# Encoder block on one core: joints of the MLP reordered and rotary angles behind the second unit of v

## The chip, the cores and the metric

The kernel runs on one core of a Trainium2 chip. The metric is the device time of one execution in microseconds (us); a lower number is better. The engines are named as the profile names them: PE is TensorE, DVE is VectorE, ACT is ScalarE, POOL is GpSimd, SP is SyncE, which here only issues DMAs.

## The reference

One encoder block over 1,024 tokens of width 1,024, in float32. `neighborhood_attention` and `dilated_attention` are softmax attentions; only the parts around the change are kept here.

```python
a = rms_norm(h, g_mix)
qa, ka, va, qd, kd, vd, gate_na, gate_dil = split(a @ w_in)
y_na  = neighborhood_attention(qa, ka, va, rpb)
y_dil = dilated_attention(rotary(qd, positions), rotary(kd, positions), vd)
mixed = sigmoid(gate_na) * (y_na @ w_branch_na) + sigmoid(gate_dil) * (y_dil @ w_branch_dil)
h = h + mixed @ w_out
c = rms_norm(h, g_mlp)
h = h + square(relu(c @ w_up)) @ w_down
e = rms_norm(h, g_ple)
h = h + sigmoid(e @ w_ple_gate) * (p @ w_ple_proj)
out = rms_norm(h, g_final)
```

## The kernel before, in words

Every matrix product is made of three passes: an operand is split into a high part (a cast on ACT, L109) and a low part (source minus high part, a subtraction on DVE or POOL, L110), and `mm3` (L206) issues high x high, high x low and low x high (profile lines L208 to L210). Weights stream through a ring of buffers (`w_raw`, `w_hi`, `w_lo`). The large products are done in blocks with seven products in place of eight: sums and differences of blocks (t1 to t4, on POOL) stand beside plain blocks (b11, b21, b22). The scheduler of the framework orders each engine's instructions from the program order, from priorities and from buffer releases; inside an engine they run in that order.

**Token tiles and v.** At the start eight token tiles of 128 rows are normalised (`norm_to_act`; L239 to L248 are small steps of the reciprocal square root, L258 writes `xn`), transposed on PE through two PSUM tiles `tp` (L275) and split into `act`. Behind them stand five units of the v projection (`v_unit`, PSUM `ps_v`, output `v_stage`). Between the tiles the rotary angles are made on DVE (L349 to L375: position times frequency, reduced to one turn by twelve steps at L358) and ACT (two Sin, L376 and L377); they are stored to `cs_scr` for the rotary step much later.

**Out-projection and first MLP product.** For each of eight token tiles, the loop at L1131 loads a row of x into `hx` (L1132), makes two halves of `mixed @ w_out` (24 matmuls each, PSUM `ps_t`), adds them (L1137) and sums squares on ACT (L234). `norm_to_ops` (L1093) of the tile before is issued behind the first half: it normalises, transposes, and for tiles 4 to 7 makes the left operands of the first MLP product: x (L1112, L1114), s2 (L1115), and two differences on POOL in `keep` (L1118, L1119), which is loaded from `c_scr` (L1106). All these are split into act10, act11, s2, s3, s4. Heads of units 0 and 1 of W_up (`fast_head`, L177: blocks b11 and b21, tile `f_raw`) and the sums of unit 0 (`fast_sums`, L183 load, L186 to L189 on POOL) are issued in the last tile. Then the loop over 16 units of W_up (L1230) makes per unit seven products of 12 matmuls (PSUM `pp`): b11 and b21, which read only tiles 0 to 3 (act00, act01), and t1, t2, t3, b22, t4, which need all tiles.

**Second MLP product.** Seven chunks of W_down (L1352 on), each seven products of four PSUM tiles `ps_d` with six matmuls each, in the order `DOWN` = b11, b21, t1, t2, t3, b22, t4. Left blocks come from `l_scr` into four places (`load_left`, L1288: two halves of `u_raw` and two of an `h` tile), right blocks from W_down (`load_right`, L1296; POOL sums at L1303). `operands` splits them for the next chunk behind each product. In chunk 0 the products b11, t1, t2, t3 are copied out of PSUM by ACT (L1339); all else is added on DVE (L1341). In the last chunk the results are combined (L1345, DVE and POOL), and the left operand of the four last units of W_up's output is split from `u_raw`: first half loaded early (L1365), the second half into the same buffer at L1380, behind the splits of the first.

**Tail.** The gate product of the last token tile is done in two pieces of 256 columns (L1434 on); each goes through `gated` (L1418 to L1423: sigmoid, times p, plus h, square), then the final norm and the store (L1454).

Of the kernel before, what the change touches and what calls it, by code (L numbers as in the profile page):

```python
# [9 lines left out]
F32 = mybir.dt.float32  # L10
# [49 lines left out]
def encoder_kernel(ctx: ExitStack, tc: tile.TileContext, t: dict, out: bass.AP):  # L60
# [236 lines left out]
    with ExitStack() as st:  # L297
# [41 lines left out]

        pi = qp.tile([P, 256], I32, name="pi", tag="rt")  # L340
        for a in range(4):
            nc.sync.dma_start(pi[a * 32:(a + 1) * 32],
                              t["positions"][:, a * 256:(a + 1) * 256].broadcast_to((32, 256)))
        invf = qp.tile([P, 1], F32, name="invf", bufs=1)
        nc.sync.dma_start(invf, t["invf"])
        hpi = qp.tile([P, 1], F32, name="hpi", bufs=1)
        nc.vector.memset(hpi, float(np.pi / 2))
        r, k1, k2, ab, sn, cn = (qp.tile([P, 256], F32, name=n_, tag="rt") for n_ in "abcdef")
        nc.vector.tensor_copy(r, pi)  # L349
        nc.vector.tensor_scalar(r, r, invf, None, op0=ALU.mult)  # L350
        big = 4096.0 * TWO_PI
        nc.vector.tensor_scalar(k1, r, 1.0 / big, MAGIC, op0=ALU.mult, op1=ALU.add)
        nc.vector.tensor_scalar(k1, k1, MAGIC, None, op0=ALU.subtract)
        cp = _fixed_parts(big, [2.0 ** (8 - 7 * i) for i in range(8)])
        pp = _fixed_parts(TWO_PI, [2.0 ** (-9 - 12 * i) for i in range(3)])

        def less(k, part, dst=r):
            nc.vector.scalar_tensor_tensor(dst, k, -part, r, op0=ALU.mult, op1=ALU.add)  # L358

        for i in range(3):  # L360
            less(k1, cp[i])
        less(k1, cp[3], k2)
        nc.vector.tensor_scalar(k2, k2, 1.0 / TWO_PI, MAGIC, op0=ALU.mult, op1=ALU.add)
        nc.vector.tensor_scalar(k2, k2, MAGIC, None, op0=ALU.subtract)
        less(k2, pp[0])
        less(k1, cp[3])
        less(k2, pp[1])
        less(k1, cp[4])
        less(k1, cp[5])
        less(k2, pp[2])  # L370
        less(k1, cp[6])
        less(k1, cp[7])
        lim = float(np.nextafter(np.float32(np.pi), np.float32(0)))
# [4 lines left out]
        for i, src in enumerate((cn, sn)):  # L378
            nc.sync.dma_start(cs_scr[i].rearrange("a f n -> (a f) n"), src)
# [42 lines left out]
        for u in range(5):  # L422
            v_unit(u)
            if u < 4:
                s1.append(left_sums(u))
# [1129 lines left out]
```

## Time and profile before

| what | value |
|---|---|
| runs | 1649.92, 1651.51, 1652.97 us; median 1651.51 us |
| profiled execution | 1654.93 us, of which the span in the trace 1653.1 us |
| PE | busy 1561.5 us, 94% of the span, 7787 instructions |
| DVE, ACT, POOL | busy 72%, 43%, 39% |
| mean granted clock of PE | 0.979 |
| DMA | 277.12 MB, mean 168 GB/s |

The profiled execution is one more run; its time is its span and 1.83 us around it. A window of the trace gives for a stretch of time how long each engine was busy and the clock that PE was granted (1.00 is 2.4 GHz, 0.50 would be 1.2 GHz throughout). A timeline gives single instructions with the idle time before them and what ended it.

### The profile page before, as it was taken

Reading aid. Unit: us, or ns where it says so; the run is one execution under the profiler, and the core shown is the slowest. Engines: PE = TensorE matmul, PEld = TensorE weight load, DVE = VectorE, ACT = ScalarE, POOL = GpSimd, SP = SyncE. Lnnn points to the kernel's source line nnn. Section 1 sums busy time; section 2 is a strip of 40 time slices with the busy share of each in tenths; the row PEclk is TensorE's granted clock in tenths of the full one; section 3 lists DMA queues with packets and bytes.
Section 4 is the critical chain, followed back from the end, with each engine's and each line's share of the span. In section 5 each row is a group of like instructions: output and inputs, shape, how many; then the busy total and the mean of one; then the engine's idle time right before and its main releaser. Section 6 shows DMA issues by size and latency. Waiting matters only on the chain. (4 is left out here: it accounts for less than half of the span.)

```text
span 1653.1 us, 22585 instructions
## 1 busy us (share of the span) xinstructions
PE 1561.5 (94%) x7787; PEld 1308.2 (79%) x7787; DVE 1193.6 (72%) x2081; ACT 708.4 (43%) x1327; POOL 652.6 (39%) x434
## 2 busy tenths in 40 slices
PE   8899999999999998889997899999989999999997
PEld 6899777787888877667786688888867788887886
DVE  6744799734666877655458777777778999999855
ACT  7322222226888755654234333333345333323422
POOL 0233578613333222234214677777733322325100
PEclk9999999999999999999998899999999999999999
DMA  8552455675676777655343344444467444434122
GB/s 295 175 152 102 126 167 162 202 259 204 207 215 225 237 240 241 182 179 162 127 166 115 115 140 147 141 147 149 162 234 267 156 163 143 153 102 139 35 101 71
DMA packets 114482, 277.12 MB, mean 168 GB/s; under 512 B 14176, under 2 KB 30528, under 8 KB 113856
## 3 DMA queue, kind: packets, MB, share of 16 engines
q1 hardware_dynamic: 108608, 265.19, 48.9%
q10 hardware_dynamic: 5760, 10.49, 1.7%
q8 instruction: 62, 1.02, 0.2%
q14 instruction: 52, 0.43, 0.1%
HBM read 185.57 MB, written 90.06 MB: 167 GB/s over the span
## 5 line engine op out<-in xcount | busy, mean ns | idle before, releaser
L109 ACT CAST w_hi<-w_raw 128x512 fp32r<-128x512 f32 (+2 forms) x103 | 83.7, 826 | 137.9 <-POOL w_raw L470 56.0
L110 POOL TENSOR_TENSOR w_lo<-w_raw,w_hi 128x512 fp32r<-128x512 f32 (+2 forms) x33 | 64.3, 1951 | 162.0 <-ACT w_hi L109 117.6
L110 DVE TENSOR_TENSOR f_lo<-f_raw,f_hi 128x512 fp32r<-128x512 f32 x80 | 81.6, 1037 | 49.2 <-ACT f_hi L109 48.6
L110 DVE TENSOR_TENSOR w_lo<-w_raw,w_hi 128x1024 fp32r<-128x1024 f32 (+1 forms) x70 | 84.2, 1209 | 36.1 <-ACT w_hi L109 35.8
L722 POOL TENSOR_SCALAR s_sb<-s_sb,rs 128x384 f32<-128x384 f32 x64 | 40.0, 626 | 136.6 <-DVE rs L721 69.1
L110 DVE TENSOR_TENSOR pt_l<-tp_p,pt_h 128x384 fp32r<-128x384 f32 (+3 forms) x120 | 65.1, 542 | 27.0 <-ACT pt_h L109 25.6
L109 ACT CAST f_hi<-f_raw 128x512 fp32r<-128x512 f32 x80 | 46.2, 614 | 79.8 <-DMA f_raw<-w_up 75.7
L109 ACT CAST pt_h<-tp_p 128x384 fp32r<-128x384 f32 (+3 forms) x120 | 56.2, 469 | 33.5 <-PE tp_p L731 27.2
L1178 POOL TENSOR_TENSOR u_t<-u_t 128x512 f32<-128x512 f32 x45 | 53.2, 1183 | 39.9 <-ACT u_t L1177 38.7
L1177 ACT ACTIVATE u_t<-u_t 128x512 f32<-128x512 f32 x45 | 28.4, 631 | 74.5 <-DVE u_t L1164 74.1
L628 POOL TENSOR_TENSOR k_lo<-k_lo,k_st 128x1024 fp32r<-128x1024 f32 x12 | 32.1, 2678 | 65.0 <-ACT k_st L625 47.0
L1341 DVE TENSOR_TENSOR h<-ps_d,h 128x512 f32<-128x512 f32 x84 | 54.7, 681 | 2.4 <-PE ps_d L210 2.2
L110 DVE TENSOR_TENSOR f_lo<-f_t,f_hi 128x512 fp32r<-128x512 f32 x32 | 51.3, 1608 | 1.8
L637 PE MATMUL sc<-k_st,q_st 128*128 128x384 f32 (+3 forms) x160 | 52.3, 327 | 0.2 <-DVE stats L655 0.2
L638 PE MATMUL sc<-k_lo,q_st 128*128 128x384 f32 (+3 forms) x160 | 49.1, 307 | 2.7 <-POOL k_lo L628 2.7
L657 ACT ACTIVATE s_sb<-s_sb,stats 128x256 f32<-128x256 f32 (+2 forms) x96 | 44.9, 469 | 14.9 <-DVE stats L655 14.4
L731 PE MATMUL tp_p<-ident,s_sb 128*128 128x128 f32 x192 | 33.9, 288 | 17.1 <-POOL s_sb L722 15.1
L647 ACT ACTIVATE s_sb<-s_sb,nm 128x384 f32<-128x384 f32 x64 | 39.5, 617 | 23.8 <-DVE nm L646 19.6
L1341 DVE TENSOR_TENSOR sum_t<-ps_d,sum_t 128x512 f32<-128x512 f32 x72 | 46.8, 682 | 2.9 <-PE ps_d L210 2.9
L731 PEld LDWEIGHTS tp_p<-ident,s_sb 128*128 128x128 f32 x192 | 25.1, 147 | 29.9 <-POOL s_sb L722 20.4
L210 PE MATMUL ps_d<-w_hi,m_op 128*128 128x512 f32 x112 | 44.3, 405 | 2.6 <-DVE m_op L110 2.6
L644 DVE CUSTOM_DVE_ANT_0 s_sb<-bias,sc 128x384 f32<-128x384 f32 x64 | 35.1, 548 | 15.8 <-PE sc L638 14.1
(482 smaller groups left out, 5809.1 us busy)
## 6 DMA issues: line engine op xcount, KB each, us to landing
f_raw<-w_up SPq DMA_DIRECT2D x32, 512.0 KB
w_raw<-w_in SPq DMA_DIRECT2D x26, 512.0 KB
u_raw<-l_scr SPq DMA_DIRECT2D x25, 512.0 KB
qk_scr<-o SPq DMA_DIRECT2D x96, 128.0 KB
h<-l_scr SPq DMA_DIRECT2D x24, 512.0 KB
l_scr<-u_t SPq DMA_DIRECT2D x42, 256.0 KB
l_scr<-u_s SPq DMA_DIRECT2D x42, 256.0 KB
w_raw<-w_qk SPq DMA_DIRECT2D x20, 512.0 KB
```

The source lines that it names most:

```text
L109: nc.scalar.copy(hi, src)
L110: eng.tensor_tensor(lo, src, hi.bitcast(F32), op=ALU.subtract)
L210: nc.tensor.matmul(ps, sl, mh, start=False, stop=last)
L637: pe(nc.tensor.matmul(o, qs[:, qsl], kk, start=True, stop=False))
L638: pe(nc.tensor.matmul(o, qs[:, qsl], ll, start=False, stop=True))
L644: nc.vector.tensor_tensor_reduce(s_[:, :n], bias, sc[:, :n], 1.0, -3.0e38, op0=ALU.subtract, op1=ALU.max, accum_out=mx)
L647: nc.scalar.activation(s_[:, :n], s_[:, :n], AF.Exp, bias=nm, scale=1.0, accum_out=sm)
L657: nc.scalar.activation(s_[:, :n], s_[:, :n], AF.Exp, bias=nm, scale=-1.0, accum_out=sm)
L722: nc.gpsimd.tensor_scalar(pr, pr, rs, 1.0, op0=ALU.mult, op1=ALU.mult)
L731: pe(nc.tensor.transpose(tp[:, i * P:(i + 1) * P], pr[:, kb * P:(kb + 1) * P], ident))
L1178: nc.gpsimd.tensor_tensor(c, c, c, op=ALU.mult)
L1341: nc.vector.tensor_tensor(d, ps, d, op=ALU.add)
```

## The change

Five pieces:

1. The angle block becomes a function `angles()` and is called behind unit 1 of v.
2. The last two token tiles of the out-projection are done by halves: tile 6 first half, tile 7 first half, then the second halves. The loads of W_up's heads stand before the second halves; `keep` of tile 7 and the raw second half of unit 0 go to two free buffers of the ring (`spare`); tiles 6 and 7 keep x in `hx`. The two last `norm_to_ops` get a higher priority, and the sums of unit 0 (`fast_sums`) come behind them. The products b11 of units 0 and 1 are issued first, then both b21.
3. Chunk 0 of the second product has the order b11, b21, b22, t1, t2, t3, t4; left blocks are loaded in that order, and the operands of chunk 1 are issued as soon as their buffers' products of chunk 0 are issued, in the order `DOWN`.
4. The second half of the last four units' output (`u_scr[2:4]`) is loaded into `m_ops[0]` behind b11 of the last chunk.
5. The last token tile's gate product is cut at 384 + 128 columns.

```diff
@@ angles: the block from "pi = qp.tile" to the stores of cs_scr, L340 to L379, becomes a function
+        def angles():
...
+            nc.vector.tensor_copy(r, pi)
...
         for u in range(5):
             v_unit(u)
+            if u == 1:
+                angles()
             if u < 4:
                 s1.append(left_sums(u))
@@ norm_to_ops
-            keep = pool.tile([P, D], F32, name="keep", tag="keep")
-            nc.sync.dma_start(keep, c_scr[r])
+            if tt == NT - 1:
+                keep = spare[0]
+            else:
+                keep = pool.tile([P, D], F32, name="keep", tag="keep")
+                nc.sync.dma_start(keep, c_scr[r])
...
-            x = xn if tt == NT - 1 else ring.tile([P, D], F32, name="x_op", tag="w_raw", bufs=2)
+            x = h if tt >= NT - 2 else ring.tile([P, D], F32, name="x_op", tag="w_raw", bufs=2)
@@ out-projection
+            def half_row(tt, n):
+                hx, parts = sums[tt]
+                ps = tok_product(w8, tt, n)
+                c = slice(n * HALF, (n + 1) * HALF)
+                nc.vector.tensor_tensor(hx[:, c], ps, hx[:, c], op=ALU.add)
+                parts.append(square_part(np_, hx[:, c], ps))
+                if n == 1:
+                    nc.sync.dma_start(h_scr[tt * P:(tt + 1) * P, :], hx)
+                    before.append((hx, g, tt, parts))
...
+            load_row(NT - 2)
+            half_row(NT - 2, 0)
+            norm_to_ops(np_, op_, *before.pop())
+            load_row(NT - 1)
+            half_row(NT - 1, 0)
+            heads = [fast_head(u) for u in range(2)]
+            spare = [ring.tile([P, D], F32R, name=f"w_{b}", tag=f"w_{b}").bitcast(F32) for b in ("hi", "lo")]
+            nc.sync.dma_start(spare[0], c_scr[3])
+            half_row(NT - 2, 1)
+            with tc.high_priority(offset=150):
+                norm_to_ops(np_, op_, *before.pop())
+                half_row(NT - 1, 1)
+                norm_to_ops(np_, op_, *before.pop())
+            late = fast_sums(0, heads[0], spare[1], op_.tile([P, D], F32, name="f_t", tag="keep"))
@@ first product, loop over units
+                if u == 0:
+                    p1[0], p1[1] = head_1(0), head_1(1)
+                    for v in range(2):
+                        head_2(v, p1[v])
                 fast_rest(heads[u], *late)
-                if u == 0:
-                    p1[0] = head(0)
...
-                if u < 14:
+                if 0 < u < 14:
                     p1[u + 1] = head(u + 1)
@@ second product
+        first_order = ("b11", "b21", "b22", "t1", "t2", "t3", "t4")
+        seq = [(0, o) for o in first_order] + [(c, o) for c in range(1, 7) for o in DOWN]
...
-            for o in DOWN:
+            due = list(DOWN)
+            for o in DOWN if c else first_order:
                 down_product(o, c == 0)
                 if c < 6:
-                    operands(c + 1, o)
+                    done = first_order[:first_order.index(o) + 1] if c == 0 else (o,)
+                    while due and due[0] in done:
+                        operands(c + 1, due.pop(0))
                     continue
-                if o == "b21":
+                if o == "b11":
+                    u_more = m_ops[0].bitcast(F32).rearrange("p (f n) -> p f n", f=2)
+                    nc.sync.dma_start(u_more, u_scr[2:4].rearrange("f p n -> p f n"))
+                elif o == "b21":
...
-                        if q:
-                            nc.sync.dma_start(u_raw, u_scr[2:4].rearrange("f p n -> p f n"))
...
-                                split(hi, lo, u_raw[:, k, half * HALF:(half + 1) * HALF].rearrange(
+                                split(hi, lo, (u_more if q else u_raw)[:, k, half * HALF:(half + 1) * HALF].rearrange(
@@ last token tile
-                for a in range(2):
-                    ps = ps_mm.tile([P, HALF], F32, name="ps_t", tag="mm")[:, :256]
-                    mm_tok(ps, w8[4:], tt, slice(a * 256, (a + 1) * 256))
+                for a, b in ((0, 384), (384, HALF)):
+                    ps = ps_mm.tile([P, HALF], F32, name="ps_t", tag="mm")[:, :b - a]
+                    mm_tok(ps, w8[4:], tt, slice(a, b))
```

The scheduler turns this into another order on the engines. Three places follow, before and then after; numbers behind a name tell buffers apart.

DVE, the middle of the token tiles: `act10l` and `act11l` are low parts of a transposed tile; L349 to L375 before (L369 to L395 after) are angles.

```order
L244 TENSOR_SCALAR nv<-nv 128x1
L358 SCALAR_TENSOR_TENSOR a<-b,a 128x256
L110 TENSOR_TENSOR w_lo<-w_raw,w_hi 128x1024
L248 SCALAR_TENSOR_TENSOR ny<-nw,ny 128x1
L247 SCALAR_TENSOR_TENSOR nw<-ny,nv 128x1
L358 SCALAR_TENSOR_TENSOR a<-b,a 128x256
L110 TENSOR_TENSOR act10l<-tp,act10h 128x512
L247 SCALAR_TENSOR_TENSOR nw<-ny,nv 128x1
L248 SCALAR_TENSOR_TENSOR ny<-nw,ny 128x1
```

```order
L247 SCALAR_TENSOR_TENSOR nw<-ny,nv 128x1
L258 SCALAR_TENSOR_TENSOR xn<-x,ny,gain 128x512 x2
L248 SCALAR_TENSOR_TENSOR ny<-nw,ny 128x1
L110 TENSOR_TENSOR w_lo<-w_raw,w_hi 128x1024
L110 TENSOR_TENSOR act10l<-tp,act10h 128x512
L242 TENSOR_SCALAR ny<-nv 128x1
L247 SCALAR_TENSOR_TENSOR nw<-ny,nv 128x1
L110 TENSOR_TENSOR act11l<-tp,act11h 128x512
L110 TENSOR_TENSOR v_stage<-ps_v,v_stage 128x8x64
```

The steps at L358 are gone from between the tiles; `angles()` starts 31 rows further down, behind a `v_stage` row of unit 1.

POOL, the joint of out-projection and first MLP product: L1118 and L1119 (L1124 and L1125 after) are the differences of a token tile, s_8965 that of tile 5, s_9069 and s_9088 those of tile 6; `f_raw_9112` is unit 0's second raw half before (`w_lo` after), `f_raw_9379` and `f_raw_9378` unit 1's.

```order
L1118 TENSOR_TENSOR keep<-keep,s_8965 128x512
L1119 TENSOR_TENSOR keep<-keep,x_op 128x512
L110 TENSOR_TENSOR s4l<-keep,s4h 128x512
L1118 TENSOR_TENSOR keep<-keep,s_9069 128x512
L1119 TENSOR_TENSOR keep<-keep,x_op 128x512
L110 TENSOR_TENSOR s4l<-keep,s4h 128x512
L186 TENSOR_TENSOR f_t<-f_raw_9112,f_raw 128x512
L186 TENSOR_TENSOR f_t<-f_raw_9379,f_raw 128x512
L187 TENSOR_TENSOR f_t<-f_raw_9112,f_t 128x512
L188 TENSOR_TENSOR f_raw_9112<-f_raw_9112 128x512
L187 TENSOR_TENSOR f_t<-f_raw_9379,f_t 128x512
L188 TENSOR_TENSOR f_raw_9379<-f_raw_9379 128x512
```

```order
L1124 TENSOR_TENSOR keep<-keep,s_8965 128x512
L1125 TENSOR_TENSOR keep<-keep,x_op 128x512
L110 TENSOR_TENSOR s4l<-keep,s4h 128x512
L186 TENSOR_TENSOR f_t<-f_raw_9378,f_raw 128x512
L187 TENSOR_TENSOR f_t<-f_raw_9378,f_t 128x512
L188 TENSOR_TENSOR f_raw_9378<-f_raw_9378 128x512
L189 TENSOR_TENSOR f_raw<-f_raw,f_t 128x512
L1124 TENSOR_TENSOR keep<-keep,s_9088 128x512
L1125 TENSOR_TENSOR keep<-keep,hx 128x512
L110 TENSOR_TENSOR s4l<-keep,s4h 128x512
L1124 TENSOR_TENSOR w_hi<-w_hi,s_9159 128x512
L1125 TENSOR_TENSOR w_hi<-w_hi,hx 128x512
```

The four sums of unit 1 moved ahead of the differences of tiles 6 and 7; the sums of unit 0 moved behind them (the row `f_t<-w_lo` follows the last one shown).

DVE, chunk 0 of the second product: L1341 (L1376 after) adds a product to its sum, `h_11724` and `h_11723` being the sum of b21, `h_11724` after that of b22.

```order
L110 TENSOR_TENSOR act11h<-u_raw,act11h 128x1024
L110 TENSOR_TENSOR act10h<-h_11723,act10h 128x1024
L110 TENSOR_TENSOR act00h<-h_11723,act00h 128x1024
L1341 TENSOR_TENSOR h_11724<-ps_d,h_11724 128x512 x4
L110 TENSOR_TENSOR m_op_11731<-u_raw,m_op_11731 128x1024
L110 TENSOR_TENSOR act10l<-t_raw,act10l 128x1024
L110 TENSOR_TENSOR w_lo<-w_raw,w_hi 128x1024
```

```order
L110 TENSOR_TENSOR act11h<-h_11722,act11h 128x1024
L110 TENSOR_TENSOR act10h<-h_11722,act10h 128x1024
L1376 TENSOR_TENSOR h_11723<-ps_d,h_11723 128x512 x4
L1376 TENSOR_TENSOR h_11724<-ps_d,h_11724 128x512 x4
L110 TENSOR_TENSOR m_op_11730<-u_raw,m_op_11730 128x1024
L110 TENSOR_TENSOR act11l<-pair,act11l 128x1024
L110 TENSOR_TENSOR w_lo<-w_raw,w_hi 128x1024
```

The four additions of b22 stand directly behind those of b21, ahead of the splits for chunk 1.

## Rows read from the trace of the kernel before

**Rows 1.** windows with the busy time of each engine (instructions), the granted clock, DMA share, GB/s.

```profile
core 0: us, PE busy (x) PEld busy (x) DVE busy (x) ACT busy (x) POOL busy (x), PEclk, DMA share, GB/s
40.00:70.00 30.00, 24.64 (x183) 23.97 (x182) 26.03 (x68) 11.54 (x21) 5.00 (x3) 0.89 0.42 133
100.00:130.00 30.00, 30.00 (x252) 30.00 (x252) 13.88 (x17) 8.86 (x14) 14.02 (x9) 1.00 0.47 151
886.00:938.00 52.00, 34.40 (x123) 25.92 (x122) 42.44 (x52) 22.02 (x40) 32.06 (x22) 0.80 0.32 106
1217.00:1268.00 51.00, 44.80 (x177) 35.60 (x176) 40.98 (x35) 28.58 (x37) 19.86 (x7) 0.90 0.70 258
1268.00:1290.00 22.00, 19.66 (x79) 14.09 (x78) 22.00 (x23) 10.56 (x11) 5.67 (x2) 1.00 0.65 218
1490.00:1510.00 20.00, 16.20 (x64) 12.59 (x62) 20.00 (x21) 3.44 (x6) 18.68 (x11) 0.91 0.38 140
```

**Rows 2.** waits of PE over the span: total us, times, longest us.

```profile
PE pp L208 <- ACT f_hi L109: 8.2, 1, 8.2
...
PE ps_d L208 <- DVE h L1341: 5.8, 4, 3.5
PE tp L275 <- DVE act10l L110: 5.3, 1, 5.3
PE pp L208 <- ACT act10h L109: 5.0, 1, 5.0
```

**Rows 3.** timeline of DVE, token tiles: start us, length us, operation, [idle before <-releaser].

```profile
39.43 0.29 DVE L349 CAST a<-pi 128x256 f32<-128x256 int32 x1 [1.04 <-DMA pi<-positions]
...
45.49 0.41 DVE L358 SCALAR_TENSOR_TENSOR a<-b,a 128x256 f32<-128x256 f32 x1
45.83 0.14 DVE L243 TENSOR_SCALAR ny<-ny 128x1 int32<-128x1 int32 x1
...
58.21 0.68 DVE L110 TENSOR_TENSOR act10l<-tp,act10h 128x512 fp32r<-128x512 f32 x1
```

**Rows 4.** timeline of SP (q: a DMA issue) around the joint of W_out and W_up.

```profile
871.36 0.33 SPq L1132 DMA_DIRECT2D hx<-x  x1
...
886.24 0.42 SPq L177 DMA_DIRECT2D f_raw<-w_up  x1
```

**Rows 5.** timeline of DVE, same stretch.

```profile
883.33 1.41 DVE L258 SCALAR_TENSOR_TENSOR xn<-hx,ny,gain 128x512 f32<-128x512 f32 x2
...
900.64 3.45 DVE L258 SCALAR_TENSOR_TENSOR xn<-hx,ny,gain 128x512 f32<-128x512 f32 x2
```

**Rows 6.** timeline of POOL, same stretch.

```profile
899.31 2.53 POOL L186 TENSOR_TENSOR f_t<-f_raw,f_raw 128x512 f32<-128x512 f32 x2 [2.15 <-DVE nw L247]
...
918.32 1.28 POOL L1118 TENSOR_TENSOR keep<-keep,s 128x512 f32<-128x512 f32 x1 [6.33 <-DVE s L1115]
```

**Rows 7.** timeline of PE, same stretch.

```profile
916.14 0.79 PE L208 MATMUL pp<-act10h,f_hi 128*128 128x512 f32 x1 [4.99 <-ACT act10h L109]
...
934.75 0.39 PE L208 MATMUL pp<-act11h,f_hi 128*128 128x512 f32 x1
...
937.47 0.39 PE L208 MATMUL pp<-act00h,f_hi 128*128 128x512 f32 x1
```

**Rows 8.** timeline of DVE, first chunk of the second product.

```profile
1240.54 2.48 DVE L1341 TENSOR_TENSOR h<-ps_d,h 128x512 f32<-128x512 f32 x4
1247.28 1.23 DVE L110 TENSOR_TENSOR m_op<-u_raw,m_op 128x1024 fp32r<-128x1024 f32 x1 [4.26 <-ACT m_op L109]
```

**Rows 9.** timeline of DVE, end of the second product.

```profile
1486.93 1.28 DVE L110 TENSOR_TENSOR act00l<-u_raw,act00h 128x512 fp32r<-128x512 f32 x2
...
1501.92 1.75 DVE L110 TENSOR_TENSOR act00l<-u_raw,act00h 128x512 fp32r<-128x512 f32 x1
```

**Rows 10.** timeline of ACT, last token tile.

```profile
1639.00 0.60 ACT L1418 ACTIVATE sg<-ps_t 128x512 f32<-128x512 f32 x1 [2.63 <-PE ps_t L210]
...
1644.75 0.38 ACT L1418 ACTIVATE sg<-ps_t 128x256 f32<-128x256 f32 x1 [0.91 <-PE ps_t L210]
```

More of the change, by code (lines that the diff above doesn't have):

```diff
@@ L337, in encoder_kernel @@
             norm_to_act(qp, two(xs[tt]), g, tt, xn=qp.tile([P, D], F32, name="xn", tag="nat"))
[L340 to L373, printed above, removed]
-        nc.vector.tensor_scalar(r, r, lim, -lim, op0=ALU.min, op1=ALU.max)
-        nc.vector.scalar_tensor_tensor(ab, r, -1.0, r, op0=ALU.mult, op1=ALU.max)
-        nc.scalar.activation(sn, r, AF.Sin)
-        nc.scalar.activation(cn, ab, AF.Sin, bias=hpi, scale=-1.0)
-        for i, src in enumerate((cn, sn)):
-            nc.sync.dma_start(cs_scr[i].rearrange("a f n -> (a f) n"), src)
         def v_unit(u):
@@ L1128, in encoder_kernel @@
             w8 = take(8, 0)
-            before = None
-            for tt in range(NT):
+            sums, before = {}, []
+            def half_row(tt, n):
[7 more added lines that the diff above has]
+                    before.append((hx, g, tt, parts))
@@ L1131, in encoder_kernel, with load_row @@
+            def load_row(tt):
                 hx = op_.tile([P, D], F32, name="hx", tag="hx", bufs=2)
                 nc.sync.dma_start(hx, t["x"][tt * P:(tt + 1) * P, :])
-                parts = []
+                sums[tt] = (hx, [])
+            for tt in range(NT - 2):
+                load_row(tt)
                 for n in range(2):
-                    ps = tok_product(w8, tt, n)
-                    c = slice(n * HALF, (n + 1) * HALF)
-                    nc.vector.tensor_tensor(hx[:, c], ps, hx[:, c], op=ALU.add)
-                    parts.append(square_part(np_, hx[:, c], ps))
-                    if before is not None and n == 0:
-                        norm_to_ops(np_, op_, *before)
-                    if tt == NT - 1 and n == 0:
-                        heads = [fast_head(u) for u in range(2)]
-                        late = fast_sums(0, heads[0], op_.tile([P, D], F32, name="f_raw2", tag="hx", bufs=2),
-                                         op_.tile([P, D], F32, name="f_t", tag="keep"))
@@ L1317, in operands @@
                 sub(r["t1"], r["b12"], r["b11"])
-            n = 7 * c + DOWN.index(o)
+            n = seq.index((c, o))
             right = {"t2": "t1", "t3": "b12", "t4": "b21"}.get(o, o)
-            for (hi, lo), src in zip(pr, (lefts.pop(n), r[right])):
+            for (hi, lo), src in zip(pr, (lefts.pop((c, o)), r[right])):
                 split(hi, lo, src)
@@ L1351, in encoder_kernel @@
                 load_left(n)
-            for o in DOWN:
+            for o in first_order:
                 operands(0, o)
```

51 lines of the change are left out of this document (44 added, 7 removed).

## Prediction

> **What bounds the kernel now.** The busy shares first: PE is busy 94% of the span, DVE 72%, so time goes wherever PE stands still or runs at a lower clock. Windows come next, cut at the four stretches the change touches and one beside them [rows 1]. Two things are read in each: what PE lacks to the length of the window, and the granted clock. A stretch at 1.2 GHz (half rate below) costs half its length, so a window of length w with mean clock c loses w × (1 − c). From 40 to 70 us PE is idle 5.36 and loses 30 × 0.11 = 3.3 to the clock: 8.7. From 886 to 938: 17.6 idle and 52 × 0.20 = 10.4, together 28. From 1217 to 1268: 6.2 and 5.1, together 11.3. From 1268 to 1290: 2.3. From 1490 to 1510: 3.8 and 1.8, together 5.6. These 56 us are all that the first four pieces can give. In 100:130 PE lacks nothing. The list of PE's waits says who ends them [rows 2]: a cast of W_up's head (8.2), DVE's low part of a token tile (5.3), the cast of the last tile (5.0), and DVE's additions out of PSUM (5.8 in four waits, 3.5 the longest). The chain of waits names only the last ACT instruction here, so it is not used; timelines of the stretches follow.
>
> **Piece 1, the angles.** PE's wait of 5.3 for act10l ends when that subtraction is done, at 58.21 + 0.68 = 58.89 [rows 2, 3]. DVE's timeline has no idle time from the first angle step at 39.43 on, which itself waited 1.04 for the positions [rows 3]. Between the two stand 13 angle steps: seven of L358, each 0.34 from its start to the next row's (45.49 to 45.83), and six smaller ones of at most 0.29, of which I count 0.2 each, since their ends overlap as in the rows [rows 3]. That is 2.4 + 1.2 + 1.04 = 4.6 that leaves the path. act10l then ends near 54.3; PE had stopped at 58.9 − 5.3 = 53.6. The wait shrinks to under 1 us, and the half rate behind it should not come: 4.6 + 3.3 = 8. Bounds: 7 if another part of the half rate stays, 8.7 if all goes. At the new place the same steps are laid on DVE while it is busy 13.9 of 30 and PE never waits [rows 1]; with ACT's two Sin and table load they hold ACT for some 7 us, and three PSUM tiles of v at 30/252 × 48 = 5.7 us each stand between ACT and PE. I cost them at nothing there; if that cover were gone, up to 4.6 would come back. On SP the four loads of positions now queue behind stores of v; only the angles wait for them. PE paces what follows, so the gain is carried on.
>
> **Piece 2, the joint.** A product of 12 matmuls takes 937.47 − 934.75 = 2.72 [rows 7]. Nine of them lie between 886 and 937.47: 24.5 us of work in 51.5. Before, the head of unit 0 is asked for at 886.24 [rows 4] and PE waits 8.2 for its cast. Now it stands on SP right behind tile 7's row of x, issued at 871.36 [rows 4], so it has landed long before PE gets there; unit 1's head waits for a buffer and lands near 890. The four heads then run from about 886.5 to 899, with two waits of a microsecond. That 8.2 is gone. But the left operands of tiles 6 and 7 are as late as before: the out-projection ends just ahead of 886 either way, tile 6's second half is now its last product, and its square sum, the small steps and both normalisations come behind it. The pair of L258 takes 1.41 alone and 3.45 beside POOL's sums [rows 5], and POOL does unit 1's four sums just then. I get both tiles transposed at 903. Behind that, POOL has five differences and casts for the two tiles and then unit 0's t1, seven operations of 1.28 each where nothing is in their way (the row at 918.32, and 2.53 for two [rows 6]), 9 us, that wait for one another, for DVE's s2 and for ACT's casts: 10 to 12 us. So t1 starts at 914.6, against 916.14 [rows 7]. PE stands idle for about 11 us in one piece instead of in three, and I count 4 for the half rate behind it, a little over the 3.3 behind the wait of 5.3, in place of the 10.4. From 914.6 five products (13.6) and 4 of half rate give 932.3, where before the next head started at 937.47: 5 us gained. Bounds: if DVE meets no POOL sums (3.45 − 1.41 = 2.0 saved twice, and two more on the POOL chain), t1 starts near 908.5 and 11 is gained; if both pairs are slowed by 2.0 and seven POOL steps by a third each (3), t1 starts near 921 and 2 is lost. I take 5, as unit 1's sums need about the time that the small steps need.
>
> Both L258 rows read two SBUF operands. The Trainium skill (SBUF — State Buffer, Who interferes with whom) says that a DVE instruction with two SBUF inputs and a GpSimd instruction that reads SBUF exclude each other for a whole instruction, whoever comes first; by that the eight POOL operations ahead of t1 would each hold DVE once, and piece 2 would give 0 to 2 instead of 5. The trace has both values, 1.41 and 3.45, so it bears the rule out without saying how many will meet.
>
> **Piece 3, the new order of chunk 0.** The wait for act10h and its half rate stay: b22's left operand, act11h, now stands third and is cast and split in the same seventh place of ACT's and DVE's lists as act10h before; 0 gained of the 11.3. What moves is four additions, 2.48 together as those of b21 [rows 8], which DVE now does in its gap of 4.26 ahead of 1247 [rows 8]; so much leaves the stretch of chunk 1, where DVE is busy 22.0 of 22 and PE lacks 2.3 [rows 1]. I take 2. Bounds: −2, if the third product's cast comes later on ACT because the load ahead of it is late, to 4.
>
> **Piece 4, the end of the second product.** DVE is busy 20 of 20 [rows 1] and the third addition of b22 comes late: 3.5 of PE's waiting [rows 2] and 1.8 of clock. Four splits leave the place ahead of it for 1479 to 1490, and one combining step moves behind it. A split there costs 1.75 beside POOL [rows 9], and at the new place a pair costs 1.28. DVE has no gap at either place, so only the difference and the combining step (1.75, as the split) count: between 0 and all 5.3 of the stretch. I take 2, since POOL has as many operations to do as before.
>
> By the same page and section the loss would be paid once for each POOL operation, whichever DVE operation meets it, and the splits' cheaper place would give nothing: 0 to 1 from the combining step alone. The two prices of the same split, 1.75 and half of 1.28, agree with a lock, not with a count of it.
>
> **Piece 5, the tail.** Sigmoid of 512 columns takes 0.60, of 256 0.38 [rows 10]. Four steps behind the last matmul (sigmoid, two on DVE, square) lose 128 columns each: 4 × 0.11 = 0.4. Bounds −0.3 (the first part's steps now reach into the second's) to 0.8.
>
> **Sum.** 8 + 5 + 2 + 2 + 0.4 = 17.4. The profiled execution took 1654.93, so 1637.5 there; it lies 3.4 above the median of 1651.51, which becomes 1634.1, and I give 1634.
>
> **Rivals.**
> - *The joint closes.* Unit 1's sums are done before the normalisation of tile 6, and t1 starts near 908.5: 6 more, 1628. For it: POOL is idle for 2.15 ahead of 899.31 [rows 6] even before. Against: unit 1's loads start only once tile 5's differences have freed a buffer. 0.17.
> - *The joint only turns its waits round.* The head waits go and the same time comes back as one wait for tiles 6 and 7: piece 2 gives −2 to 1, and 1640. For it: the price of 3.45. 0.2. The page's lock, paid by every operation, is this rival.
> - *Something else ends the wait at 59.* If the next row of x, not DVE, holds the tile, piece 1 gives 3 and all of it 1639. Against: DVE has no gap there. 0.06.
> - *Slower.* SP's list: head and raw half of unit 1, `keep` of tile 6, `spare` for tile 7 and unit 0's raw half are five loads behind one wait for tile 5's differences. Each microsecond by which they come late moves t1. The other pieces give 12.4, so the kernel is slower by over 3.3 only where t1 starts after 914.6 + 5 + 12.4 + 3.3 = 935, with loads landing 20 us later than I walk them. 0.05.
>
> **How the numbers follow.** My forecast has 0.52. 0.2% is 3.3 us, about what runs of this kernel can tell from no change. The ends of all bounds add to 1622 and 1649; the range 1623 to 1646 leaves out the slower rival and the corners. Faster takes the forecast and the first three rivals but for their late corners: 0.88; same 0.06; slower 0.06.
>
> **What would show it.** Window 40:70 at a clock near 1.00 and no wait for act10l over 1 us; no wait of 8 for f_hi at the joint, but one near 10 ahead of t1, and the head of unit 2 some 13 us earlier than 937.47 (8 from piece 1, 5 from piece 2); the wait for act10h of 1.9 now one for act11h; DVE's longest wait at the end of the second product under 2. I am wrong if PE waits between 80 and 110, if t1 is later against the end of the out-projection than now, or if the time is above 1646.

## The result and the profile after

| | before | after |
|---|---|---|
| runs, us | 1649.92 to 1656.13, median of 6: 1652.24 | 1634.67 to 1644.20, median of 6: 1640.31 |
| profiled execution, span | 1654.93, 1653.1 | 1643.55, 1641.8 |
| PE busy, mean granted clock | 1561.5, 0.979 | 1555.5, 0.982 |

The ratio is 0.9923, with a 95% interval of 0.9898 to 0.9948: 12 us faster, where 17.4 were forecast. The time of 1640 lies in the range, but the way to it is not the one that was forecast. By the traces about 7 come from piece 1, 2 from piece 3, 2 from pieces 4 and 5, and nothing or a small loss from piece 2, though it did at the joint what the prediction said. These add to 9 to 11, within the interval of 8.6 to 16.9.

Windows of the kernel after, with the columns of [rows 1]. Each lies at about the place of the program that a window of [rows 1] shows; where PE stands still less, more matmuls fall into it (155 in place of 123 at the joint). The second window alone has no such partner: it is where the angles now run.

```profile
core 0: us, PE busy (x) PEld busy (x) DVE busy (x) ACT busy (x) POOL busy (x), PEclk, DMA share, GB/s
40.00:70.00 30.00, 29.15 (x247) 28.95 (x246) 23.20 (x50) 12.69 (x21) 8.00 (x4) 1.00 0.67 208
70.00:100.00 30.00, 30.00 (x252) 30.00 (x251) 23.86 (x39) 10.69 (x17) 10.46 (x6) 1.00 0.64 172
870.00:922.00 52.00, 36.02 (x155) 27.50 (x153) 43.69 (x63) 22.32 (x42) 30.14 (x21) 0.87 0.30 101
1210.00:1261.00 51.00, 44.27 (x176) 35.21 (x175) 46.59 (x37) 28.88 (x37) 20.66 (x7) 0.90 0.74 272
1258.00:1280.00 22.00, 20.48 (x91) 16.61 (x90) 21.87 (x24) 11.01 (x12) 5.69 (x2) 1.00 0.69 220
1480.00:1500.00 20.00, 17.51 (x74) 13.29 (x73) 20.00 (x23) 1.86 (x2) 19.02 (x11) 1.00 0.29 93
```

The token tiles run at clock 1.00 and PE lacks 0.85 in place of 5.36; the new place of the angles (DVE's first step at 78.58, the last Sin at 89.85) costs PE nothing: from 70 to 100 it is busy throughout. At the joint the clock is 0.87 in place of 0.80. At the end of the second product PE lacks 2.5 in place of 3.8, at clock 1.00.

Waits of PE over the span in the kernel after, with the columns of [rows 2].

```profile
PE pp L208 <- ACT f_hi L109: 12.2, 2, 11.0
...
PE pp L208 <- DVE part L1192: 5.5, 11, 1.5
PE ps_d L208 <- ACT act11h L109: 3.6, 1, 3.6
...
PE tp L275 <- DVE act10l L110: 0.9, 1, 0.9
```

The wait for act10l is down to 0.9, and that of the second product for act10h has become one for act11h. The 11.0 for f_hi is the one wait ahead of t1 that was forecast. One line is new and was in no part of the prediction: eleven waits for `part`, the DVE additions that empty PSUM in the units of W_up. The kernel before has no wait of PE at all in that loop.

Timeline of PE in the kernel after, from the joint into the units of W_up.

```profile
877.75 0.51 PE L210 MATMUL pp<-act00h,f_lo 128*128 128x512 f32 x1 [1.49 <-DVE f_lo L110]
881.49 0.51 PE L208 MATMUL pp<-act00h,f_hi 128*128 128x512 f32 x1 [1.14 <-ACT f_hi L109]
904.14 0.80 PE L208 MATMUL pp<-act10h,f_hi 128*128 128x512 f32 x1 [11.02 <-ACT f_hi L109]
921.37 0.39 PE L208 MATMUL pp<-act00h,f_hi 128*128 128x512 f32 x1
...
945.31 0.47 PE L208 MATMUL pp<-act01h,f_hi 128*128 128x512 f32 x1 [1.48 <-DVE part L1192]
965.05 0.47 PE L208 MATMUL pp<-act01h,f_hi 128*128 128x512 f32 x1 [0.42 <-DVE part L1192]
...
1210.80 0.39 PE L208 MATMUL ps_d<-w_hi,m_op 128*128 128x512 f32 x1
```

Ahead of the joint the program is 9.7 earlier than before (the out-projection's first matmul, at 792.78 before, stands at 783.07); some 7 of it are piece 1's, the rest is scatter between executions. At t1 it is 12.0 earlier (916.14 to 904.14), at unit 2's head 16.1 (937.47 to 921.37), and at the first matmul of the second product, which stood at 1217.93, only 7.1. So nine microseconds are lost between unit 2 and the end of W_up's loop, in a stretch that the prediction did not look at. The experiments ask why.

### The profile page after: what moved, and what is told of

It is laid out like the page before. It is cut to its first block, busy times and chain, and to the rows that moved or that the text cites. A ratio compares the mean times of both kernels' runs of the same rounds, so it can differ in the third digit from the quotient of the medians.

```text
span 1641.8 us, 22581 instructions
## 1 busy us (share of the span) xinstructions
PE 1555.5 (95%) x7787; PEld 1303.3 (79%) x7787; DVE 1199.1 (73%) x2081; ACT 707.6 (43%) x1327; POOL 656.5 (40%) x434
## 5 line engine op out<-in xcount | busy, mean ns | idle before, releaser
L725 POOL TENSOR_SCALAR s_sb<-s_sb,rs 128x384 f32<-128x384 f32 x64 | 39.9, 625 | 134.4 <-DVE rs L724 71.7
L1376 DVE TENSOR_TENSOR h<-ps_d,h 128x512 f32<-128x512 f32 x84 | 54.1, 680 | 2.3 <-PE ps_d L210 2.2
L1376 DVE TENSOR_TENSOR sum_t<-ps_d,sum_t 128x512 f32<-128x512 f32 x72 | 46.6, 680 | 2.3 <-PE ps_d L210 2.3
```

The lines of the kernel that those rows point to most:

```text
L725: nc.gpsimd.tensor_scalar(pr, pr, rs, 1.0, op0=ALU.mult, op1=ALU.mult)
L1376: nc.vector.tensor_tensor(d, ps, d, op=ALU.add)
```

## The experiments

Two theories stood against each other. **A:** the right operands of W_up's units have a loop of their own: load `f_raw`, sums on POOL, casts and splits, buffer free, next load. It turns in 19.6 us, PE's seven products in 19.04. Before, PE came so late that this never showed; a PE that comes earlier only finds the slower loop. **B:** the five pieces add up as forecast, and the waits belong to this one build. From the fifth run on the rival is **C:** the waits come from DVE's list or PE's own turn, whatever the loads do.

The kernel before alone already shows the loop. Timelines of SP, POOL and DVE in the kernel before, one turn.

```profile
977.01 0.33 SPq L183 DMA_DIRECT2D f_raw<-w_up  x1
...
978.46 0.33 SPq L177 DMA_DIRECT2D f_raw<-w_up  x1
...
996.41 0.33 SPq L183 DMA_DIRECT2D f_raw<-w_up  x1
...
983.85 1.30 POOL L186 TENSOR_TENSOR f_t<-f_raw,f_raw 128x512 f32<-128x512 f32 x1 [2.61 <-DMA f_raw<-w_up]
...
984.37 1.32 DVE L110 TENSOR_TENSOR f_lo<-f_raw,f_hi 128x512 fp32r<-128x512 f32 x1 [2.40 <-ACT f_hi L109]
...
987.33 3.47 DVE L110 TENSOR_TENSOR f_lo<-f_t,f_hi 128x512 fp32r<-128x512 f32 x2
990.72 0.68 DVE L1164 TENSOR_TENSOR part<-pp,p 128x512 f32<-128x512 f32 x1
...
994.65 1.72 DVE L110 TENSOR_TENSOR f_lo<-f_raw,f_hi 128x512 fp32r<-128x512 f32 x2 [0.61 <-ACT f_hi L109]
```

From the load (977.01) to POOL's first sum 6.84, from there to the first addition `part` 6.87, from there to the next load, behind the split that frees f_raw, 5.69: a turn of 19.40. Over the eleven turns from 957.36 to 1173.54 the landing lies between 6.37 and 7.70; the other two terms are 6.85 to 6.88 and 5.68 to 5.69 in every turn. The mean is 19.65. DVE's list is not full: it stands idle for 2.40 ahead of the first split of the turn (984.37), whose cast waits for the landing. But the addition stands in the list behind these splits, so PSUM comes free at the loop's pace. At its start that does not matter and at its end it nearly does. Timelines of DVE and PE in the kernel before, an early and a late unit.

```profile
951.67 0.68 DVE L1164 TENSOR_TENSOR part<-pp,p 128x512 f32<-128x512 f32 x1
...
1167.85 0.68 DVE L1164 TENSOR_TENSOR part<-pp,p 128x512 f32<-128x512 f32 x1
...
956.51 0.39 PE L208 MATMUL pp<-act00h,f_hi 128*128 128x512 f32 x1
975.55 0.39 PE L208 MATMUL pp<-act00h,f_hi 128*128 128x512 f32 x1
...
1166.17 0.39 PE L208 MATMUL pp<-act00h,f_hi 128*128 128x512 f32 x1
```

The addition starts 4.8 ahead of PE's next head in the first of these units and 1.7 behind it in the last; PE uses up 6.5 of slack, at 19.04 a unit (956.51 to 975.55), and gets through without a wait. In the kernel after, PE enters with that slack gone: at 961.75 it starts a head, the addition follows at 964.23, 2.5 behind, and PE waits.

All runs at a glance; "loop" is from unit 2's head to the first matmul of the second product, "turn" the mean from one load of f_raw to the next behind unit 2's head, "waits" those of PE for DVE's additions out of PSUM in the loop. All us.

| run | ratio to before (95%) | unit 2's head | loop | turn | waits (times) |
|---|---|---|---|---|---|
| before | 1 | 937.47 | 280.46 | 19.65 | 0 |
| after | 0.9923 (0.9898 to 0.9948) | 921.37 | 289.43 | 19.65 | 5.5 (11) |
| e1_angles | 0.9936 (0.9916 to 0.9956) | 926.57 | 280.64 | 19.68 | 0 |
| e2_joint | 1.0009 (0.9994 to 1.0024) | 927.63 | 289.06 | 19.65 | 5.3 (11) |
| e3_rest | 0.9958 (0.9943 to 0.9973) | 936.12 | 280.16 | 19.54 | 0 |
| e4_nojoint | 0.9923 (0.9901 to 0.9946) | 926.65 | 280.96 | 19.63 | 0.5 (1) |
| e5_loop | 1.0006 (0.9993 to 1.0019) | 918.96 | 301.64 | 20.07 | 14.2 (18) |
| e6_loop_nojoint | 0.9997 (0.9985 to 1.0008) | 927.18 | 293.70 | 20.19 | 8.5 (14) |
| e7_free | 0.9943 (0.9925 to 0.9961) | 923.71 | 288.09 | 19.81 | 4.1 (11) |
| e8_free_nojoint | 0.9923 (0.9906 to 0.9941) | 925.36 | 285.14 | 20.02 | 2.2 (6) |
| e9_adds | 0.9893 (0.9878 to 0.9907) | 920.52 | 280.49 | 18.64 | 0 |
| e10_adds_nojoint | 0.9926 (0.9910 to 0.9943) | 927.92 | 280.16 | 19.22 | 0 |
| e11_chunk0 | 0.9989 (0.9976 to 1.0002) | 932.22 | 281.71 | 19.79 | 0.8 (2) |
| e12_ends | 1.0001 (0.9988 to 1.0014) | 934.39 | 281.24 | 19.65 | 0.7 (1) |

### The pieces by themselves

**e1_angles**: the kernel before with the angle block moved behind unit 1 of v.

```diff
+            if u == 1:
+                angles()
```

> The kernel before with piece 1 alone (the angles behind unit 1 of v). Theory A (a second loop): in the loop over W_up's units the loads of f_raw, POOL's sums and the casts behind them turn in 19.6 us, PE's seven products in 19.04; before, PE entered that loop late and used up some 7 us of slack over twelve units, so the end of the loop moves only with its first loads. Piece 1 moves everything behind it alike, the loads too: -8.5, 1643 to 1645, and no wait of PE for the additions (part) over 0.5 us in the units of W_up. Theory B (the pieces simply add up as predicted and the W_up waits of the whole change are an accident of that build): -8, the same time. Both fall if the angles give under 6.

Measured 1642.68 against 1653.58, 10.9 less, with no wait in the units. Both theories hold here. By the trace the first matmul behind v comes 153.56 behind the program's first matmul, against 159.29 before; 150.39 in the whole change and 150.92 in e4_nojoint: 5.7 to 8.9 gained. Over all kernels the mean is 159.0 for the five with the old place of the angles and 151.8 for the nine with the new one: 7.3.

**e2_joint**: the kernel before with piece 2 alone (the out-projection's last two tiles by halves, early heads, both b11 and then both b21).

```diff
+            half_row(NT - 2, 0)
...
+            half_row(NT - 1, 0)
+            heads = [fast_head(u) for u in range(2)]
...
+            half_row(NT - 2, 1)
```

> The kernel before with piece 2 alone (the joint between the out-projection and W_up). Theory A: PE reaches unit 2's first product some 6 us earlier than before, but the loads of f_raw turn no earlier (1 to 3 us later, as they came 1.7 to 2.5 less early than PE ahead of the joint in the whole change), so that PE waits for the additions from the units in the middle of the loop on and all 6 are given back: 0 to +2.5, 1652 to 1655. Theory B: -5, 1647, and no waits in the units.

Measured 1655.07, 1.0009: no gain, and 5 are excluded. Waits and timeline of PE in e2_joint, from unit 2's head on.

```profile
PE pp L208 <- DVE part L1189: 5.3, 11, 1.3
...
927.63 0.39 PE L208 MATMUL pp<-act00h,f_hi 128*128 128x512 f32 x1
...
1216.69 0.39 PE L208 MATMUL ps_d<-w_hi,m_op 128*128 128x512 f32 x1
```

Unit 2's head is 9.84 earlier than before (937.47); the out-projection's first matmul came 3.48 earlier in this execution too (789.30 and 792.78), so 6.4 are the joint's, as in the whole change. At the second product the kernel is only 1.24 earlier (1217.93): not only the 6.4 are given back but 2.2 more. Theory A expected 0 to 2.5 of loss. B is out.

**e3_rest**: the kernel before with pieces 3, 4 and 5.

```diff
+        first_order = ("b11", "b21", "b22", "t1", "t2", "t3", "t4")
...
+                    nc.sync.dma_start(u_more, u_scr[2:4].rearrange("f p n -> p f n"))
...
+                for a, b in ((0, 384), (384, HALF)):
```

> The kernel before with pieces 3, 4 and 5 (order of chunk 0, early load of u_more, cut of the tail). Both theories: -4 to -4.5, 1648: the longest wait at the end of the second product under 2 instead of 3.5, and 2 us less between the start of chunk 0 and that of chunk 2. If the two gains overlap (DVE paces the whole second product), -2, 1650.

Measured 1646.67 against 1653.58; the interval is 4.5 to 9.4 us. The trace gives 3.9 for the three pieces together (below, e11_chunk0 and e12_ends); the rest of the 6.9 is within the scatter of the runs (1641.47 to 1650.51).

**e4_nojoint**: the whole change without piece 2.

> The whole change without piece 2 (pieces 1, 3, 4, 5). Theory A: piece 2 gives nothing at the end of the W_up loop or costs 1 to 2 there, so this kernel takes the time of the whole change or is 1 to 2 faster: 1638 to 1640; the head wait of 8 us is back and the units show no waits for part over 0.5. Theory B: 5 slower than the whole change, 1645.

Measured 1639.81, ratio 0.9923 as the whole change. Piece 2 is worth nothing in the whole change; A again, and B would have had 1645.

### What the loop's turn decides

**e5_loop** and **e6_loop_nojoint**: sums and splits of unit u+2 ahead of the additions of unit u, with and without piece 2.

```diff
+                for v in {0: (1,), 1: (2, 3)}.get(u, (u + 2,)):
...
+                        t3, b22, t4s[v] = sums_of(v)
+                        fast_rest_f(heads[v], t3, b22)
...
+                u2 = plus(ps["t2"], p1, pin=1 < u < 14)
```

> The whole change with another order inside the W_up loop: the sums of unit u+2 and the two splits of t3 and b22 that give its buffer f_raw back stand ahead of the additions and the first Relu of unit u, in place of behind them, so that the next load can be issued some 3 us earlier in each turn. Theory A (the loop load, sums, splits, next load turns in 19.6 us and holds PE, which needs 19.04): the loads follow at PE's 19.04, the waits for part go, the loop ends 6 to 9 earlier: 1632 to 1635. Theory C (PE, now earlier, waits because DVE's additions themselves come late in DVE's list): the two splits ahead of them, 1.7 to 1.8 a pair, make every wait longer, 10 to 20 in the loop: 1650 to 1660.

> The same order inside the W_up loop, on the whole change without piece 2 (the kernel of the fourth run). Theory A: PE did not wait there, so a faster loop of loads gives nothing, 0 to -1: 1639 to 1640; with it piece 2 would now be worth what was predicted of it, 5 to 7 between this run and the fifth. Theory C: as with piece 2 or a little less, 0 to 10 slower.

Measured 1655.39 and 1652.02. The edit missed: the turn became longer, not shorter. By number the result lies where C put it, and e6_loop_nojoint, where A expected no change, is 12 slower. Timelines of SP and ACT in e5_loop, one turn.

```profile
1005.03 0.33 SPq L183 DMA_DIRECT2D f_raw<-w_up  x1
...
1026.27 0.33 SPq L183 DMA_DIRECT2D f_raw<-w_up  x1
...
1023.34 0.63 ACT L1212 ACTIVATE u_a<-u_a 128x512 f32<-128x512 f32 x1 [5.80 <-DVE u_a L1197]
```

The next load is now issued 0.1 behind the start of the first addition (1026.16), but from landing to addition it takes 13.70 in place of 6.87: the casts of t3 and b22 now stand on ACT behind the Relu of u_a, which waits 5.80 for a DVE list into which sums of left blocks have slipped between the splits. So the two runs don't tell A and C apart. They show one thing: PE enters the loop 8.2 later in e6_loop_nojoint (927.18 and 918.96) and reaches the second product at the same time (1220.88 and 1220.60). The end of a loop that turns in 20.1 does not depend on when PE enters it.

**e7_free** and **e8_free_nojoint**: t3 goes into the head's own buffer, b22 is split first, so that f_raw comes free one split earlier; with and without piece 2.

```diff
-        nc.gpsimd.tensor_tensor(b12, b22, b12, op=ALU.subtract)
+        nc.gpsimd.tensor_tensor(b11, b22, b12, op=ALU.subtract)
...
-        fast_split(fp, "f", 2, (("t3", t3), ("b22", b22)), ops)
+        fast_split(fp, "f", 2, (("b22", b22), ("t3", t3)), ops)
```

> The whole change, with t3 written into the first half of the head's own buffer (b11's, no longer needed) in place of b12's, and b22 split ahead of t3. The load buffer f_raw is then given back behind the low part of b22, one DVE split (0.85 us in the traces) earlier in each turn; the engines' lists stay as they are but for u_a one place later on DVE. Theory A: the turn of the loads falls from 19.65 to 18.8, under PE's 19.04, the waits for part die out behind the first units, the W_up loop ends 5 to 8 earlier than in the whole change: 1632 to 1635. Theory C (the waits belong to DVE's list, not to the loads): no change, 1640, or 1 slower by the later u_a.

> The same edit on the whole change without piece 2. Theory A: the loads turn at 18.8 to 19.04, but PE did not wait for them there: 1639 to 1640 as the fourth run; so piece 2 is worth 5 to 8 between this run and the seventh. Theory C: 1639 to 1641 here, and no difference between the two.

Measured 1643.11 and 1640.46: again no gain, and A's price wrong again. Timelines of SP and POOL in e7_free.

```profile
1007.02 0.33 SPq L183 DMA_DIRECT2D f_raw<-w_up  x1
...
1009.07 0.33 SPq L177 DMA_DIRECT2D f_raw<-w_up  x1
...
1015.51 1.29 POOL L186 TENSOR_TENSOR f_t<-f_raw,f_raw 128x512 f32<-128x512 f32 x1 [3.65 <-DMA f_raw<-w_up]
```

The last term of the turn fell as meant, from 5.69 to 5.09, but the landing rose from a mean of 7.1 to 7.9. POOL's first sum is b12 minus b11 and needs both loads of the unit, f_raw (L183) and the head (L177). The head's load was issued 1.45 behind the other before (978.46 and 977.01) and is now issued 2.05 behind: it waits for the split of t4, which the edit left where it was. So the first load was freed earlier and the second was not. These runs, too, leave C standing.

**e9_adds** and **e10_adds_nojoint**: in place of the loads, the additions are taken out of the turn: DVE's splits of unit u+1's head are queued behind the first two additions of unit u-1, which until now stood behind them and so behind a load. With and without piece 2.

```diff
-                    heads.append(fast_head(u + 1))
+                    with tc.issue_after(added[u - 1]) if u > 1 else ExitStack():
+                        heads.append(fast_head(u + 1))
...
                 u4 = plus(ps["t1"], u2)
+                added[u] = last[0]
```

> The whole change, with DVE's splits of unit u+1's head (two low parts of f_raw, which wait for the load) queued behind the first two additions of unit u-1 (the sums out of t2 and t1), so that these additions, whose products are long done, no longer stand behind a load. In the trace of the whole change a turn of the loads is landing (6.5 to 7.5) + 6.87 to the first addition + 5.69 to the next load. Theory A: three operations of 0.65 leave the middle of the turn for DVE's idle place ahead of the landing, and the casts of t3 and b22 no longer wait for a Relu (0.6): the turn falls to about 17, below PE's 19.04; PSUM comes free earlier, no wait for part over 0.3 from the second turn on, units 19.04 apart, the W_up loop ends 7 to 9 earlier than in the whole change: 1631 to 1634. Theory C (PE's turn itself grew, by its own lower rate or by products that are missing operands): no change, 1640.

> The same edit on the whole change without piece 2. Theory A: PE did not wait there but for 0.5, so nothing is gained: 1639 to 1640; piece 2 is then worth 5 to 8, between this run and the ninth, as predicted of it, where it was worth 0 before. Theory C: 1639 to 1640 here too, but no difference between the two.

Measured 1634.02 and 1639.19. Timelines of DVE and PE in e9_adds.

```profile
970.86 0.69 DVE L1194 TENSOR_TENSOR u_a<-pp,p 128x512 f32<-128x512 f32 x1 [0.20 <-DVE u_t L1221]
971.47 0.68 DVE L1194 TENSOR_TENSOR part<-pp,p 128x512 f32<-128x512 f32 x1
972.19 0.69 DVE L1194 TENSOR_TENSOR part<-pp,part 128x512 f32<-128x512 f32 x1
973.24 3.03 DVE L110 TENSOR_TENSOR f_lo<-f_raw,f_hi 128x512 fp32r<-128x512 f32 x2 [0.36 <-ACT f_hi L109]
976.19 3.47 DVE L110 TENSOR_TENSOR f_lo<-f_t,f_hi 128x512 fp32r<-128x512 f32 x2
...
920.52 0.39 PE L208 MATMUL pp<-act00h,f_hi 128*128 128x512 f32 x1
...
1201.01 0.39 PE L208 MATMUL ps_d<-w_hi,m_op 128*128 128x512 f32 x1
```

u_a and the first two additions stand where DVE waited for the landing before; 0.36 of that wait is left. The four turns from 947.78 on take 17.6 to 18.1, PE does not wait once in the loop, which takes 280.49 as in the kernel before, and the whole is 0.9893 of before, 18.2 us faster; its interval (0.9878 to 0.9907) lies below the whole change's 0.9923, though it overlaps that one's interval. Against e10_adds_nojoint, run beside it, the runs themselves do not overlap: its five lie between 1632.11 and 1636.61, the six without piece 2 between 1637.30 and 1644.01. Without piece 2 the same edit gives nothing (0.9926), since PE did not wait there. With it piece 2 is worth 1639.19 - 1634.02 = 5.2, the 5 that were forecast for it; from the out-projection's first matmul to the second product the traces give 5.8 (418.77 and 424.58). So PE's own turn had not grown, and A stands with one thing added from C: the loads pace PE only through the additions that stood behind them in DVE's list. PE's operands themselves were never late. The ninth kernel is the one to keep.

### The small pieces

**e11_chunk0**: piece 3 alone. **e12_ends**: pieces 4 and 5 alone. Their edits are the first and the last two lines of e3_rest's.

> The kernel before with piece 3 alone (order of chunk 0 of the second product). The first prediction's term is 2, between -2 and 4: the wait for act10h (1.88, then 1.69 behind it) becomes one of the same length for act11h, and the waits at the start of chunk 1's third products shrink, since four additions of b22 are done ahead. Its rival, that the time is only moved to the third product, gives 0. Time 1650 to 1652; the trace decides by the distance from the first matmul of the second product to the first of chunk 2, against the same in the kernel before.

> The kernel before with pieces 4 and 5 (early load of u_more; the tail cut at 384 and 128). The first prediction's terms are 2 (0 to 5.3) and 0.4 (-0.3 to 0.8): the wait of 3.5 at the end of the second product shrinks to under 2, 1649.5 to 1650. Rival (a lock between DVE and POOL that is paid once for each POOL operation wherever the splits stand): 0 to 1, 1651.5.

Measured 0.9989 (0.9976 to 1.0002) and 1.0001 (0.9988 to 1.0014): two microseconds are at the edge of what twelve runs can tell, so the traces decide. From the first matmul of the second product to the first of chunk 2 four kernels with the old order took 90.1 to 91.9 (before, e1, e2, e12), four with the new 89.0 to 89.8 (after, e3, e4, e11): 1.9 between the means, with a scatter of the old ones as wide. All of it lies in chunk 1, where the two groups stand apart: from its first matmul to that of chunk 2 it is 40.5 to 42.7 and 39.6 to 39.9. From the first matmul of chunk 3 to the end of the program kernels without pieces 4 and 5 took 305.2 to 305.3 (before, e1, e11), those with them 303.3 (after, e3, e12): 2.0. Timelines of PE and of ACT in the tail of the kernel after.

```profile
1626.76 0.33 PE L208 MATMUL ps_t<-w_hi,act10h 128*128 128x384 f32 x1
1626.93 0.34 PE L209 MATMUL ps_t<-w_lo,act10h 128*128 128x384 f32 x1
...
1631.12 0.27 PE L210 MATMUL ps_t<-w_hi,act10l 128*128 128x128 f32 x1
1631.23 0.28 PE L208 MATMUL ps_t<-w_hi,act10h 128*128 128x128 f32 x1
...
1633.83 0.28 ACT L1458 ACTIVATE sg<-ps_t 128x128 f32<-128x128 f32 x1 [0.30 <-PE ps_t L210]
```

The last Sigmoid takes 0.28 in place of 0.38 [rows 10] and the steps behind the last matmul are 0.5 shorter. But matmuls of 128 columns start 0.11 apart, and those of 256 columns in the kernel before started 0.12 apart (1638.74, 1638.86): half the columns, nearly the same time. The 24 of 384 columns take 4.18 and the 24 of 128 take 2.63, 6.81 against 48 x 0.12 = 5.76. So piece 5 gives 0.5 and costs 1.05: from the first matmul of these pieces to the end of the program it is 15.0 in place of 14.4, 0.6 slower. The two pieces together give 2.0, so piece 4 gives 2.6.

## Why the prediction was right or wrong

**Piece 1, right.** 8 forecast, 7.3 seen in the mean, 5.7 to 8.9 in single traces. The wait for act10l shrank to 0.9, the half rate went, and the new place cost nothing. That place was misjudged: the window of [rows 1] that was read for it begins at 100, the angles run from 78.58 on. DVE is busy 23.86 of 30 there, in place of the 13.9 that were counted on, and PE still did not wait. ACT's part, two Sin and a table load, took 2.1 from 88.23 on, where some 7 were counted.

**Piece 2, right at the joint, wrong as a term of the sum.** The step that failed is "From 914.6 five products (13.6) and 4 of half rate give 932.3, where before the next head started at 937.47: 5 us gained", taken into the sum as if what follows would carry it on, as was said of piece 1. In the prediction's base, 9.7 later than the trace after, t1 came at 913.8 (forecast 914.6) and unit 2's head at 931.1 (forecast 932.3): 6.4 gained, and the idle time ahead of t1 was 11.02 (forecast about 11). Then the loop gave 9.0 back (289.43 - 280.46): 5.5 of it PE's waits for the additions, the rest some 0.3 for each of the eleven, which I read as PE filling again. In the runs the kernels with and without piece 2 do not differ, 0.9923 each. Piece 1 moves the loop's loads with everything else, so its gain is carried; piece 2 moves PE earlier and the loads later. Timelines of PE and SP in the kernel before and in the kernel after: the out-projection's first matmul and the load of unit 3's sums.

```profile
792.78 0.47 PE L208 MATMUL ps_t<-w_hi,act00h 128*128 128x512 f32 x1 [1.43 <-DVE gt L1064]
...
936.87 0.33 SPq L183 DMA_DIRECT2D f_raw<-w_up  x1
```

```profile
783.07 0.47 PE L208 MATMUL ps_t<-w_hi,act00h 128*128 128x512 f32 x1 [1.42 <-DVE gt L1067]
...
930.20 0.33 SPq L183 DMA_DIRECT2D f_raw<-w_up  x1
```

The load comes 144.1 behind that matmul before and 147.1 after. In the six kernels with the old order of the loop and without piece 2 (before, e1, e3, e4, e11, e12) it is 143.6 to 144.8, in e2_joint 146.75. The load ahead of it, unit 2's, is issued at 912.64, when two splits of f_raw end (911.29, 1.28); these now stand behind those of f_t (four at 904.12, 6.64 together), unit 0's among them, and so behind tiles 6 and 7. From this load to the second product it is 280.6 in both kernels with piece 2 and 280.8 to 282.3 in the six without: the end of the loop goes with the load. So by the traces piece 2 costs about 2: from the out-projection's first matmul to the second product 427.7 and 427.4 with it, 425.0 to 426.7 without. The runs cannot tell this from nothing. An order that frees that buffer earlier was not tried.

A row that said so was there to read: the window of the loop shows PE without a wait, but the loads' own period, 19.65 by SP's rows, is longer than PE's 19.04. Slack that shrinks by 0.6 a unit over twelve units is a bound, though no wait shows it.

Within the joint two sizes were off and cancelled. The pairs of L258 were not slowed by POOL (1.41 and 1.42 in the trace after), where I had taken 3.45 as in [rows 5]: unit 1's sums were done ahead of them. That was the rival "the joint closes", and its 6 us did not follow: POOL then stood still for 5.78 in the middle, waiting for DVE's s2, and t1 came only 0.8 earlier than forecast. That 914.6 was so near is in part luck. The two bounds around it also count the same 2.0 a pair twice, as a gain in one and as a loss in the other.

**Piece 3, right.** 2 forecast, 1.9 seen, and in chunk 1 as forecast; the wait for act11h (3.63) is that for act10h (1.88 and 1.69) with another name.

**Piece 4, right in direction, a little low.** 2 forecast, 2.6 seen; the wait of 3.5 is gone and the longest are 1.14 and 1.01. The Trainium skill (SBUF — State Buffer, Who interferes with whom) says that a DVE instruction with two SBUF inputs and a GpSimd instruction that reads SBUF keep each other out; by my reading of it this piece would give 0 to 1. The rows of the W_up loop agree with the rule itself: the pair of f_lo out of f_t takes 3.47 beside POOL's sums, 1.7 each, while `part`, which reads one operand from PSUM, takes 0.68 with POOL at work. What I made of it was too little. The four splits took 5.84 together before; two timeline rows of DVE in the kernel after show them at the new place.

```profile
1472.25 2.38 DVE L110 TENSOR_TENSOR act10l<-m_op,act10h 128x512 fp32r<-128x512 f32 x2
...
1479.96 0.68 DVE L110 TENSOR_TENSOR act00l<-m_op,act00h 128x512 fp32r<-128x512 f32 x1
```

With the fourth (0.68 too) they take 3.74: POOL had been idle there for 7.50, up to 1480.98.

**Piece 5, wrong in sign.** +0.4 forecast, -0.6 seen, outside the bounds given. The step that failed is "Four steps behind the last matmul (sigmoid, two on DVE, square) lose 128 columns each": it is right (0.5), but the matmuls themselves were counted by their columns, and a matmul of 128 columns costs nearly what one of 256 does.

**The sum.** 17.4 forecast, 11.9 measured. Without the 5 of piece 2, and with -0.6 in place of 0.4 for piece 5, the sum would have been 11.4. So 1640 lies in the range because the range was wide, not because the sum held.

The rival "the joint only turns its waits round" gave 1640, and the time is 1640, but its mechanism was not what happened: the joint itself gained 6.4, and the time came back in another place. "Slower" by SP's list did not come: t1 was not late.

## What to carry to other kernels

Ahead of forecasting that a gain is carried on, look at the next loop for a period of its own: take the issue times of its loads over ten turns and divide, and compare with PE's. A loop that is slower than PE but starts with slack shows no wait at all, and swallows the gain that brings PE closer to it. Where an in-order engine holds work that empties PSUM behind work that waits for a load, queue the first ahead; that was worth 5 to 6 us here, about half the whole change's gain.

## What the runs showed of the hardware

- PE's matmuls of 128 x 128 weights and float32 columns start 0.227 us apart at 512 columns, 0.174 at 384, 0.120 at 256 and 0.111 at 128 (last token tile, before and after, at a granted clock of 1.00). The weight loads of these rows are one for each matmul and keep the same distance of 0.11. The Trainium skill (TensorE: Matmul & The Clock Gate, LDWEIGHTS (loading the stationary operand)) gives a load the number of its columns divided by 1.2 in nanoseconds, an estimate of 107 ns for 128 columns; the 0.111 us of the last rows agrees.
- The turn of the loop is rigid: with the old order of DVE's list the two terms behind the landing stay within 0.03 us in every turn, 6.85 to 6.88 and 5.68 to 5.69 (before, after, e4_nojoint). All the scatter of a turn (18.9 to 20.3) is in the time from the load's issue to POOL's first sum, which needs two loads of 512 KB.
